# The end of a layer norm in another order: chain to the reciprocal first, means behind it, low parts tile by tile, first new products over two tiles at once

## The chip, the cores and the metric

The kernel runs on one core of one Trainium2 chip. A core has a matrix engine (TensorE, "PE" in the profile), a vector engine (VectorE, "DVE"), an activation engine (ScalarE, "ACT"), a general engine (GpSimd, "POOL") and a queue that only issues transfers (SyncE, "SP"). Each engine works through its own queue in order, and the engines wait for each other by semaphores. The metric is the device time of one execution in microseconds; smaller is better.

## The reference

One inference step of a streaming encoder for two request groups, 256 new frames of one stream and 64 frames of another, of width 1024. Each of two layers computes, with the same weights for both groups:

```python
x = layer_norm(ALPHA * x + 0.5 * swiglu(x, f1_w1, f1_w2), ln1_g, ln1_b)
z = x @ w_in                      # latents, band q k v, gates
...                               # latent attention and chunked band attention
mix = (sigmoid(g_a) * (o_a @ w_pa) + sigmoid(g_b) * (o_b @ w_pb)) @ w_out
x = layer_norm(ALPHA * x + mix, ln2_g, ln2_b)
x = layer_norm(ALPHA * x + 0.5 * swiglu(x, f2_w1, f2_w2), ln3_g, ln3_b)
```

```python
def layer_norm(x, g, b):
    mu = mean(x); var = mean((x - mu) ** 2)
    return (x - mu) * rsqrt(var + NORM_EPS) * g + b
```

All in float32. So there are six layer norms in a row of dependent stages, and nothing behind a norm can be computed wholly before it.

## The kernel before

**Layout.** The 320 frames (64 + 256) lie along the free axis and the 1024 features along the partitions, in eight tiles of 128 x 320. A mean over the features is therefore a product with a matrix of ones divided by 1024 (`self.ones`), which leaves the mean in every partition.

**Three products for one.** Each float32 factor is split into a high part in a shorter format that the matrix engine takes at full rate and a low part, the rest. `mm3` (L125) makes one product of a weight block and an activation tile from three: high with high, high weight with low activation, low weight with high activation.

**Weights.** All weights come in one stream of 128 x 128 blocks in the order of use (`WeightStream`, L49). A transfer on SP's queue brings eight blocks; ACT casts them to the high part `whi` (L81) and DVE subtracts to get `wlo` (L82). Each call of `next` keeps three chunks loaded and two split ahead. Eight blocks feed 24 products. The order of the blocks in memory is recorded from the order of the calls.

**A layer norm** (`layer_norm`, L309) has the tiles of ALPHA*x + f(x) in `d[0..7]`, made one after the other by `produce(m)`. All values are shifted by a first estimate `c` of the mean, taken from tile 0. `S` sums the tiles and `Q` their squares. `finished(m)` makes, for all but the last norm, a "raw" pair (high and low part of d times the gain, not normalised), then squares the tile on ACT and adds it to `Q` on DVE.

**The group.** While mean and variance are worked out, PE multiplies the raw pairs with the weights of the next stage's first six output tiles (`ffn_group`, L220, or `mix_group`, L232; six accumulators, 8 x 6 x 3 = 144 products). Two added columns of the raw pairs carry gain and bias, so that `finish` (L242) can correct the results later: `fin = (md * u + ps) * rstd` on DVE, with `u` copied out of the accumulator.

**The end of a norm** before the change, in the order of the source: the group's first step (18 products with raw tile 0); `pm` and `pq`, the products of ones with `S` and `Q`; `msq` (square of `pm`, ACT); the variance and its clamp (DVE L384, L385); the square root (ACT L386); the reciprocal (DVE L387); `md`, a copy of `pm`; the other steps of the group; the mean taken off all eight tiles (DVE L396, read from the accumulator `pm`); then for each tile the scaling by gain and reciprocal (DVE L399), the high part `xhi` with the bias (ACT L404) and the low part `xlo` (DVE L405). The last norm makes no raw pairs and no low parts; it writes its tiles out, and POOL takes the mean off three of them.

**Behind the norm.** `ffn` evacuates the group's three pairs of accumulators (`evac`, with `finish`) and multiplies the other 19 pairs from `xhi` and `xlo`, in each pair first all eight blocks of one accumulator and then those of the other. `attention` takes the group's results as band q, band k and latent kv, and starts with the four tiles of band v (`w_in("bv", i, "mm")`). It also adds `xhi` and `xlo` on POOL for the next residual (`residual`, L305), which the FFN does on DVE.

**Accumulators.** Eight banks in two pools of four, tagged "mm" and "at". The group holds three of each; `pm` takes the fourth "at" and `pq` the fourth "mm".

**The order on each engine** is planned when the program is built: a planner places the instructions by priority, which is the order of the source, as soon as its own estimate of times says that their inputs are ready. `high_priority()` moves what stands inside it ahead. `order(ins, after)` (L110) adds an edge that only holds for this planning and makes no semaphore: `ins` is placed behind `after` on its queue.

Of the kernel before, what the change touches and what calls it, by code (L numbers as in the profile page):

```python
# [8 lines left out]
F32 = mybir.dt.float32  # L9
F32R = mybir.dt.float32r  # L10
AF = mybir.ActivationFunctionType
ALU = mybir.AluOpType
# [3 lines left out]
T = 320  # L16
# [3 lines left out]
KD = D // P  # L20
# [14 lines left out]
TR = T + 2  # L35
# [65 lines left out]
class Model:  # L101
# [23 lines left out]
    def mm3(self, out, w, x, start, stop):  # L125
        self.mm(out, w[0], x[0], start, False)
        self.mm(out, w[0], x[1], False, False)
        self.mm(out, w[1], x[0], False, stop)

    def scratch(self, name="t"):  # L130
        return self.sc.tile([P, T], F32, tag="t", name=name)
# [88 lines left out]
    def ffn_group(self, l, f):  # L220
        NG = 3
        grp = [[self.psum("mm"), self.psum("at")] for _ in range(NG)]

        def step(k, x, n):
            for p in range(NG):
                for j in range(2):
                    w = self.ws.next(("w1", l, f, p, j, k))
                    self.mm3(grp[p][j][:, :n], w, x, k == 0, k == KD - 1)

        return grp, step  # L230

    def mix_group(self, l):  # L232
        grp = [self.psum("mm" if j < 3 else "at") for j in range(6)]

        def step(k, x, n):
            for j in range(6):
                what, i = (("bq", 0), ("bk", 0), ("bq", 1), ("bk", 1), ("ckv", 0), ("ckv", 1))[j]
                self.mm3(grp[j][:, :n], self.ws.next((what, l, i, k)), x, k == 0, k == KD - 1)

        return grp, step  # L240

# [12 lines left out]
    def ffn(self, l, f, pre):  # L254
        tc, nc, ws = self.tc, self.nc, self.ws
        which = 1 if f == 1 else 3
        last = l == DEPTH - 1 and which == 3
        with tc.tile_pool(name="h", bufs=1, reuse_waits="tile") as hp, \
# [18 lines left out]
            grp = pre  # L277
# [2 lines left out]
            self.raw_pre = True  # L280
            for p in range(len(grp), KF):
                pair = (self.psum("mm"), self.psum("at"))
                for j in range(2):
                    for k in range(KD):
                        w = ws.next(("w1", l, f, p, j, k))
                        self.mm3(pair[j][:, :T], w, (self.xhi[k], self.xlo[k]), k == 0, k == KD - 1)
                evac(p, *pair, False)

            def produce(m):
# [19 lines left out]
    def layer_norm(self, l, which, dd, sums, raw, produce, ys, group):  # L309
# [3 lines left out]
        nc = self.nc  # L313
        last = group is None
        c, S, Q = sums
# [8 lines left out]
                nc.gpsimd.tensor_copy(raw[m][0][:, T:TR], self.csth[:, g])  # L324
                nc.gpsimd.tensor_copy(raw[m][1][:, T:TR], self.cstl[:, g])

        def finished(m):

            if not last:
                g = gain[m][0]  # L330
                nc.scalar.activation(raw[m][0][:, :T], d[m], AF.Copy, scale=g)
                nc.vector.scalar_tensor_tensor(raw[m][1][:, :T], d[m], g, raw[m][0].bitcast(F32)[:, :T], ALU.mult, ALU.subtract)
            if m == 0:
                nc.scalar.activation(Q, d[0], AF.Square)
            elif not (last and m == KD - 1):
                q = self.scratch("sq")
                nc.scalar.activation(q, d[m], AF.Square)
                nc.vector.tensor_tensor(Q, Q, q, ALU.add)

        ps = produce(0)  # L340
        nc.vector.scalar_tensor_tensor(d[0], d[0], scale, ps[:, :T], ALU.mult, ALU.add)
# [7 lines left out]
        finished(0)  # L349
        for m in range(1, KD):  # L350
# [4 lines left out]
            if m == KD - 1:  # L355
                nc.vector.tensor_tensor(S, S, d[m], ALU.add)
                nc.vector.tensor_tensor(S, S, ps[:, :T], ALU.add)
            nc.vector.tensor_tensor(d[m], d[m], ps[:, :T], ALU.add)
            if m < KD - 1:
                nc.vector.tensor_tensor(S, d[0] if m == 1 else S, d[m], ALU.add)  # L360
            finished(m)
        sq = None
        if last:
            sq = self.scratch("sq")
            nc.scalar.activation(sq, d[KD - 1], AF.Square)
        else:
            grp, step = group()
            step(0, raw[0], TR)
        pm = self.psum("at", "pm")
        pq = self.psum("mm", "pq")  # L370
        self.mm(pm[:, :T], self.ones, S, True, True)
        self.mm(pq[:, :T], self.ones, Q, True, not last)
        if last:
            self.mm(pq[:, :T], self.ones, sq, False, True)
        md, v = self.md, self.rstd
        msq = self.scratch("msq")
        if not last:
            warm = self.scratch("warm")
            nc.scalar.activation(warm[:, 0:2], self.ones[:, 0:2], AF.Sqrt)
        nc.scalar.activation(msq, pm[:, :T], AF.Square)  # L380
        if last:
            nc.vector.scalar_tensor_tensor(v, pq[:, :T], eps, msq, ALU.add, ALU.subtract)
        else:
            nc.vector.tensor_tensor(v, pq[:, :T], msq, ALU.subtract)  # L384
            nc.vector.tensor_scalar(v, v, 0.0, eps, ALU.max, ALU.add)  # L385
        nc.scalar.activation(v, v, AF.Sqrt)  # L386
        nc.vector.reciprocal(v, v)  # L387
        nc.scalar.copy(md, pm[:, :T])
        if not last:
            for k in range(1, KD):  # L390
                step(k, raw[k], TR)
        for m in range(KD):
            if last and m in (4, 5, 6):
                nc.gpsimd.tensor_tensor(d[m], d[m], md, ALU.subtract)
            else:
                nc.vector.tensor_tensor(d[m], d[m], pm[:, :T], ALU.subtract)  # L396
        for m in (0, 1, 2, 3, 7, 4, 5, 6) if last else range(KD):
            g, b = gain[m]
            nc.vector.scalar_tensor_tensor(d[m], d[m], g, v, ALU.mult, ALU.mult)  # L399
            if last:  # L400
                nc.scalar.activation(d[m], d[m], AF.Identity, bias=b)  # L401
                nc.sync.dma_start(out=self.a["y"][:, m, :], in_=d[m])
            else:
                nc.scalar.activation(self.xhi[m], d[m], AF.Identity, bias=b)  # L404
                nc.vector.scalar_tensor_tensor(self.xlo[m], d[m], b, self.xhi[m].bitcast(F32), ALU.add, ALU.subtract)  # L405
        return None if last else grp


    def mixer(self, l, pre):
# [29 lines left out]
class Mixer:  # L439
# [328 lines left out]
    def attention(self, pre):  # L768
# [265 lines left out]
```

## Time and profile before

| | |
|---|---|
| time, median of 3 runs | 1524.67 us (1524.53 to 1528.79) |
| the profiled execution, its own time | 1524.2 us |
| its span, first to last instruction | 1522.4 us |
| granted clock of the matrix engine, mean | 0.990 |
| products | 10204 |

The page gives the time by engine, the chain of work that ended last, and the costliest groups of instructions; a line number is that of the listing above, and all products have the line of `mm` (L108). In a row of the timeline stand start, length, engine, line, operation, output and inputs, shapes, count, and in brackets how long the engine had been idle and what released it. In a row of the stretches stand the stretch, its length, the busy time of each engine with its instructions, the clock granted to PE, the share of the transfer engines and GB/s. In a row of the waits stand who waited for whom, how long in total, how often, and the longest.

### The profile page before, as it was taken

What the parts mean: (1) busy time and instruction counts of PE and PEld (TensorE: products, weight loads), DVE (VectorE), ACT (ScalarE), POOL (GpSimd) and SP (SyncE); (2) the same over time, 40 slices, a digit from 0 to 9 for tenths busy, and PEclk for the clock granted to TensorE, in tenths of its full rate; (3) what the DMA queues carried; (4) which work ended last, traced back from release to release, by engine and by line L of the source; (5) the groups of instructions that cost most, each with busy time, mean ns of one, the idle gap of its engine ahead of it and who ended that gap; (6) DMA issues with size and microseconds to landing.
All of it is one profiled execution on the core that took longest, in us unless ns stands there. A gap on an engine that the chain in (4) does not pass through costs nothing.

```text
span 1522.4 us, 25515 instructions
## 1 busy us (share of the span) xinstructions
PE 1488.9 (98%) x10204; PEld 1453.5 (95%) x10204; DVE 932.7 (61%) x1571; ACT 713.4 (47%) x1190; POOL 105.6 (7%) x194
## 2 busy tenths in 40 slices
PE   9999999999999989999999999999999998999996
PEld 9999999999899989999999999989998998999996
DVE  6444558774566884446595445597655579744454
ACT  5344334665444554444454444357634445444332
POOL 2000002231002000000010000042110000000000
PEclk9999999999999999999999999999999999999998
DMA  7544443854234434454444544457352254444541
GB/s 244 150 152 152 148 147 123 256 152 130 88 97 126 152 111 150 144 150 152 153 141 150 152 152 145 149 156 223 126 148 83 84 153 139 126 152 152 151 144 59
DMA packets 69910, 219.37 MB, mean 144 GB/s; under 512 B 8416, under 2 KB 17568, under 8 KB 69792
## 3 DMA queue, kind: packets, MB, share of 16 engines
q1 hardware_dynamic: 69792, 217.75, 46.4%
q8 instruction: 80, 1.31, 0.4%
q14 instruction: 38, 0.31, 0.1%
HBM read 211.74 MB, written 4.67 MB: 142 GB/s over the span
## 4 chain that ended last, share of the span: by engine, by line
PE 95%; DVE 3%; ACT 1%; issue 0%; DMA 0%; ACTq 0%; DVEq 0%
PE ps L108 89%; PE sp L108 1%; PE po L108 1%; PE ss L108 1%; DVE d L399 1%; DVE wlo L82 1%; DVE xlo L405 1%; PE st L549 0%; DVE rstd L387 0%; ACT d L401 0%; DVE d L396 0%; DMA wst<-in_w_dram 0%; PE pt L556 0%; PE st L552 0%; PE pt L555 0%
## 5 line engine op out<-in xcount | busy, mean ns | idle before, releaser
L82 DVE TENSOR_TENSOR wlo<-wst,whi 128x1024 fp32r<-128x1024 f32 (+1 forms) x387 | 471.7, 1220 | 384.6 <-ACT whi L81 382.9
L81 ACT CAST whi<-wst 128x1024 fp32r<-128x1024 f32 (+1 forms) x387 | 402.4, 1041 | 495.4 <-PE ps L108 233.6
L108 PE MATMUL ps<-xhi,whi 128*128 128x320 f32 x1760 | 548.8, 313 | 11.5 <-DVE fin L249 5.8
L108 PE MATMUL ps<-xlo,whi 128*128 128x320 f32 x1760 | 549.0, 312 | 6.7 <-DVE xlo L405 6.7
L108 PE MATMUL ps<-xhi,wlo 128*128 128x320 f32 x1760 | 545.0, 311 | 0.0
L108 PEld LDWEIGHTS ps<-xhi,whi 128*128 128x128 f32 x1760 | 333.2, 190 | 13.8 <-issue 6.8
L108 PEld LDWEIGHTS ps<-xlo,whi 128*128 128x128 f32 x1760 | 333.6, 190 | 9.5 <-DVE xlo L405 8.5
L108 PEld LDWEIGHTS ps<-xhi,wlo 128*128 128x128 f32 x1760 | 332.8, 190 | 0.6 <-issue 0.5
L108 PE MATMUL ps<-hh,whi 128*128 128x320 f32 x704 | 217.6, 309 | 0.0
L108 PE MATMUL ps<-hh,wlo 128*128 128x320 f32 x704 | 217.5, 309 | 0.0
L108 PE MATMUL ps<-hl,whi 128*128 128x320 f32 x704 | 217.5, 309 | 0.0
L108 PEld LDWEIGHTS ps<-hh,whi 128*128 128x128 f32 x704 | 132.2, 188 | 0.0
L108 PEld LDWEIGHTS ps<-hh,wlo 128*128 128x128 f32 x704 | 132.1, 188 | 0.0
L108 PEld LDWEIGHTS ps<-hl,whi 128*128 128x128 f32 x704 | 132.1, 188 | 0.0
L138 ACT CAST hh<-h 128x320 fp32r<-128x320 f32 x88 | 39.9, 456 | 62.0 <-DVE h L273 57.2
L273 DVE TENSOR_TENSOR h<-silu,ps 128x320 f32<-128x320 f32 x79 | 38.0, 484 | 49.0 <-PE ps L108 49.0
L145 DVE TENSOR_TENSOR hl<-h,hh 128x320 fp32r<-128x320 f32 x88 | 42.5, 488 | 17.5 <-ACT hh L138 17.4
L272 ACT ACTIVATE silu<-ps 128x320 f32<-128x320 f32 x79 | 33.9, 433 | 25.7 <-PE ps L108 25.7
L108 PE MATMUL ps<-rawl,whi 128*128 128x322 f32 x144 | 45.5, 316 | 0.0
L108 PE MATMUL ps<-rawh,whi 128*128 128x322 f32 x144 | 45.4, 315 | 0.0
L108 PE MATMUL ps<-rawh,wlo 128*128 128x322 f32 x144 | 44.7, 311 | 0.0
L108 PE MATMUL ps<-raw,whi 128*128 128x322 f32 x192 | 44.3, 316 | 0.0
(247 smaller groups left out, 1794.7 us busy)
## 6 DMA issues: line engine op xcount, KB each, us to landing
wst<-in_w_dram SPq DMA_DIRECT2D x382, 512.0 KB, 3.5
K<-in_ckT_dram SPq DMA_DIRECT2D x8, 256.0 KB, 4.7
vc<-in_cv_dram SPq DMA_DIRECT2D x8, 256.0 KB, 5.1
T<-in_E_dram SPq DMA_DIRECT2D x16, 128.0 KB, 3.9
xin<-in_x_dram SPq DMA_DIRECT2D x8, 160.0 KB, 5.7
out_kb_dram<-K SPq DMA_DIRECT2D x8, 160.0 KB, 3.7
out_vb_dram<-vt SPq DMA_DIRECT2D x8, 160.0 KB, 5.0
out_y_dram<-d SPq DMA_DIRECT2D x8, 160.0 KB, 1.9
```

Of the source, the lines that this page charges most:

```text
L81: self.nc.scalar.copy(hi[:, a:b], t[:, a:b])
L82: self.nc.vector.tensor_tensor(lo[:, a:b], t[:, a:b], hi.bitcast(F32)[:, a:b], ALU.subtract)
L108: return self.nc.tensor.matmul(out, lhsT, rhs, start=start, stop=stop)
L138: self.nc.scalar.copy(out, src)
L145: eng.tensor_tensor(out, src, hi.bitcast(F32), ALU.subtract)
L272: nc.scalar.activation(s, pa[:, :T], AF.Silu)
L273: nc.vector.tensor_tensor(h, s, pg[:, :T], ALU.mult)
L399: nc.vector.scalar_tensor_tensor(d[m], d[m], g, v, ALU.mult, ALU.mult)
L405: nc.vector.scalar_tensor_tensor(self.xlo[m], d[m], b, self.xhi[m].bitcast(F32), ALU.add, ALU.subtract)
```

## The change

The end of `layer_norm` is reordered; the computation stays the same.

- `finished(m)` is divided into `raw_part(m)` and `square(m)`. For the last tile the sum `S`, the tile itself and its square (with the sum `Q`) come first, at high priority, and the raw part behind them.
- `pm`, `pq`, the warming of the square root's table, `md`, `msq`, variance, clamp, square root and reciprocal are at high priority. `pq` is placed behind the last product of the group's first step (`step` and `mm3` return it). `msq` is the square of `md`, no longer of `pm`.
- The mean is taken off with `md` in place of `pm` (all norms but the last), and from the third tile on (in the last norm from the first) it is placed behind the clamp (`begun`).
- Scaling, high part and low part follow tile by tile: the scaling of tile m is placed behind the low part of tile m-2.
- The first pair of products behind the group in `ffn` goes through the eight tiles of x once, with both accumulators in turn, and so do the first two tiles of band v in `attention`.

```diff
     def mm3(self, out, w, x, start, stop):
...
-        self.mm(out, w[1], x[0], False, stop)
+        return self.mm(out, w[1], x[0], False, stop)
...
                 pair = (self.psum("mm"), self.psum("at"))
-                for j in range(2):
-                    for k in range(KD):
-                        w = ws.next(("w1", l, f, p, j, k))
-                        self.mm3(pair[j][:, :T], w, (self.xhi[k], self.xlo[k]), k == 0, k == KD - 1)
+                both = [(j, k) for k in range(KD) for j in range(2)] if p == len(grp) else [(j, k) for j in range(2) for k in range(KD)]
+                for j, k in both:
+                    w = ws.next(("w1", l, f, p, j, k))
+                    self.mm3(pair[j][:, :T], w, (self.xhi[k], self.xlo[k]), k == 0, k == KD - 1)
...
-        def finished(m):
-
+        def raw_part(m):
             if not last:
                 g = gain[m][0]
                 nc.scalar.activation(raw[m][0][:, :T], d[m], AF.Copy, scale=g)
                 nc.vector.scalar_tensor_tensor(raw[m][1][:, :T], d[m], g, raw[m][0].bitcast(F32)[:, :T], ALU.mult, ALU.subtract)
...
+        def square(m):
+            q = Q if m == 0 else self.scratch("sq")
+            nc.scalar.activation(q, d[m], AF.Square)
+            if m and not (last and m == KD - 1):
                 nc.vector.tensor_tensor(Q, Q, q, ALU.add)
+            return q
...
+        m = KD - 1
+        ps = produce(m)
+        nc.vector.tensor_tensor(S, S, d[m], ALU.add)
+        with self.tc.high_priority():
+            nc.vector.tensor_tensor(S, S, ps[:, :T], ALU.add)
+            nc.vector.tensor_tensor(d[m], d[m], ps[:, :T], ALU.add)
+            sq = square(m)
+        raw_part(m)
+        after = None
+        if not last:
             grp, step = group()
-            step(0, raw[0], TR)
+            after = step(0, raw[0], TR)
...
+        with self.tc.high_priority():
+            self.mm(pm[:, :T], self.ones, S, True, True)
+            ins = self.mm(pq[:, :T], self.ones, Q, True, not last)
+            if last:
+                self.mm(pq[:, :T], self.ones, sq, False, True)
+            else:
+                self.order(ins, after)
+                warm = self.scratch("warm")
+                nc.scalar.activation(warm[:, 0:2], self.ones[:, 0:2], AF.Sqrt)
+            nc.scalar.copy(md, pm[:, :T])
+            nc.scalar.activation(msq, md, AF.Square)
+            if last:
+                begun = nc.vector.scalar_tensor_tensor(v, pq[:, :T], eps, msq, ALU.add, ALU.subtract)
+            else:
+                nc.vector.tensor_tensor(v, pq[:, :T], msq, ALU.subtract)
+                begun = nc.vector.tensor_scalar(v, v, 0.0, eps, ALU.max, ALU.add)
+            nc.scalar.activation(v, v, AF.Sqrt)
+            nc.vector.reciprocal(v, v)
         if not last:
             for k in range(1, KD):
                 step(k, raw[k], TR)
...
-                nc.vector.tensor_tensor(d[m], d[m], pm[:, :T], ALU.subtract)
...
+                ins = nc.vector.tensor_tensor(d[m], d[m], pm[:, :T] if last else md, ALU.subtract)
+                if last or m >= 2:
+                    self.order(ins, begun)
...
+        low = []
+        for m in range(KD):
+            g, b = gain[m]
+            ins = nc.vector.scalar_tensor_tensor(d[m], d[m], g, v, ALU.mult, ALU.mult)
+            if m >= 2:
+                self.order(ins, low[m - 2])
+            nc.scalar.activation(self.xhi[m], d[m], AF.Identity, bias=b)
+            low.append(nc.vector.scalar_tensor_tensor(self.xlo[m], d[m], b, self.xhi[m].bitcast(F32), ALU.add, ALU.subtract))
+        return grp
...
+        two = [M.psum("mm"), M.psum("at")]
+        for k in range(KD):
+            for i in range(2):
+                M.mm3(two[i][:, :T], ws.next(("bv", l, i, k)), self.x[k], k == 0, k == KD - 1)
         pv = [M.psum("at") for _ in rows]
         for i in range(NPAIR):
-            ps = self.w_in("bv", i, "mm")
+            ps = two[i] if i < 2 else self.w_in("bv", i, "mm")
```

More of the change, by code (lines that the diff above doesn't have):

```diff
@@ L227, in step @@
                     w = self.ws.next(("w1", l, f, p, j, k))
-                    self.mm3(grp[p][j][:, :n], w, x, k == 0, k == KD - 1)
+                    ins = self.mm3(grp[p][j][:, :n], w, x, k == 0, k == KD - 1)
+            return ins
         return grp, step
@@ L237, in step @@
                 what, i = (("bq", 0), ("bk", 0), ("bq", 1), ("bk", 1), ("ckv", 0), ("ckv", 1))[j]
-                self.mm3(grp[j][:, :n], self.ws.next((what, l, i, k)), x, k == 0, k == KD - 1)
+                ins = self.mm3(grp[j][:, :n], self.ws.next((what, l, i, k)), x, k == 0, k == KD - 1)
+            return ins
         return grp, step
@@ L332, in finished @@
                 nc.vector.scalar_tensor_tensor(raw[m][1][:, :T], d[m], g, raw[m][0].bitcast(F32)[:, :T], ALU.mult, ALU.subtract)
[L333 to L337, printed above, removed]
+        def square(m):
+            q = Q if m == 0 else self.scratch("sq")
+            nc.scalar.activation(q, d[m], AF.Square)
+            if m and not (last and m == KD - 1):
                 nc.vector.tensor_tensor(Q, Q, q, ALU.add)
+            return q
         ps = produce(0)
@@ L348, in layer_norm @@
         nc.vector.tensor_tensor(d[0], d[0], c, ALU.subtract)
-        finished(0)
-        for m in range(1, KD):
+        raw_part(0)
+        square(0)
+        for m in range(1, KD - 1):
             if last and m == KD - 2:
@@ L354, in layer_norm @@
             ps = produce(m)
-            if m == KD - 1:
-                nc.vector.tensor_tensor(S, S, d[m], ALU.add)
-                nc.vector.tensor_tensor(S, S, ps[:, :T], ALU.add)
             nc.vector.tensor_tensor(d[m], d[m], ps[:, :T], ALU.add)
[L359 to L366, printed above, removed]
+            nc.vector.tensor_tensor(S, d[0] if m == 1 else S, d[m], ALU.add)
@@ L367, in layer_norm @@
+            raw_part(m)
+            square(m)
+        m = KD - 1
[5 more added lines that the diff above has]
+            sq = square(m)
+        raw_part(m)
+        after = None
+        if not last:
             grp, step = group()
-            step(0, raw[0], TR)
+            after = step(0, raw[0], TR)
@@ L369, in layer_norm @@
         pm = self.psum("at", "pm")
         pq = self.psum("mm", "pq")
[L371 to L374, printed above, removed]
         md, v = self.md, self.rstd
         msq = self.scratch("msq")
[L377 to L388, printed above, removed]
+        with self.tc.high_priority():
[16 more added lines that the diff above has]
+            nc.vector.reciprocal(v, v)
@@ L395, in layer_norm @@
             else:
[L396 to L400, printed above, removed]
+                ins = nc.vector.tensor_tensor(d[m], d[m], pm[:, :T] if last else md, ALU.subtract)
+                if last or m >= 2:
+                    self.order(ins, begun)
+        if last:
+            for m in (0, 1, 2, 3, 7, 4, 5, 6):
+                g, b = gain[m]
+                nc.vector.scalar_tensor_tensor(d[m], d[m], g, v, ALU.mult, ALU.mult)
                 nc.scalar.activation(d[m], d[m], AF.Identity, bias=b)
                 nc.sync.dma_start(out=self.a["y"][:, m, :], in_=d[m])
[L403 to L406, printed above, removed]
+            return None
+        low = []
+        for m in range(KD):
+            g, b = gain[m]
+            ins = nc.vector.scalar_tensor_tensor(d[m], d[m], g, v, ALU.mult, ALU.mult)
[4 more added lines that the diff above has]
+        return grp
     def mixer(self, l, pre):
```

## The prediction

> **What bounds the kernel now.** I read the page first, then the waits of the matrix engine (PE), then the timeline around each of the six norms.
>
> ```profile
> PE 1488.9 (98%) x10204; PEld 1453.5 (95%) x10204; DVE 932.7 (61%) x1571; ACT 713.4 (47%) x1190; POOL 105.6 (7%) x194
> PE 95%; DVE 3%; ACT 1%; issue 0%; DMA 0%; ACTq 0%; DVEq 0%
> 5.01 169.42 PE ps L108 x1150
> ```
>
> The first row is the busy time by engine, the second the chain that ended last by engine, the third one piece of that chain: start, length, what. PE is the bound: 169.42 us for 1150 products is 0.147 us a product, and no product is added or removed by the change. Only the holes in PE's work can be won. I number the norms N1 to N6 in order of time; N1 and N4 hand over to the mixers, N2 and N5 to the second FFNs, N3 to the next layer, N6 ends the kernel. The waits of PE, asked for one norm at a time (us in total, times, longest), are for N1
>
> ```profile
> PE ps L108 <- DVE xlo L405: 2.2, 1, 2.2
> PE ps L108 <- DVE fin L249: 1.2, 1, 1.2
> ```
>
> for N2
>
> ```profile
> PE ps L108 <- ACT xhi L404: 3.8, 1, 3.8
> PE ps L108 <- DVE xlo L405: 3.1, 1, 3.1
> ```
>
> for N4
>
> ```profile
> PE ps L108 <- DVE fin L249: 1.8, 1, 1.8
> PE ps L108 <- DVE xlo L405: 1.5, 4, 0.4
> ```
>
> and for N5
>
> ```profile
> PE ps L108 <- DVE fin L249: 2.8, 1, 2.8
> PE ps L108 <- ACT xhi L404: 1.7, 1, 1.7
> ```
>
> N3 has none. They sum to 3.4, 6.9, 3.3 and 4.5, so 18.1 us. Behind each hole the granted clock falls. The stretches by window show it (length, PE busy, granted clock, DMA, GB/s):
>
> ```profile
> 266.00:272.00 6.00, 4.82 (x17) 0.50 0.94 306
> 544.00:549.00 5.00, 4.59 (x18) 0.53 0.00 0
> 1023.00:1027.00 4.00, 4.00 (x19) 0.57 0.06 15
> 1294.00:1300.00 6.00, 5.50 (x21) 0.53 0.28 89
> ```
>
> Busy time times the missing share of the clock gives 4.82 x 0.50 = 2.4, then 2.2, 1.7 and 2.6: 8.9 us. So N1 costs 5.8, N2 9.1, N4 5.0, N5 7.1, N3 nothing: **27.0 us is all there is to win**, 1.8% of the time. The Trainium skill's page "TensorE: Matmul & The Clock Gate", Part 1, puts the fall to half clock behind an idle window of about 3.4 us; the 3.8 us hole of N2 agrees, but N4 lost its clock with no hole above 1.8 us, so here the measurement decides and thinly filled stretches count too.
>
> **What the waits are made of.** N2 shows the chain best. The products from the unnormalised tiles (the group of 144) end at 536.7; the next ones need xhi and xlo.
>
> ```profile
> 524.06 0.56 ACT L331 ACTIVATE raw<-d,cst 128x320 fp32r<-128x320 f32 x1
> 525.34 0.55 DVE L332 SCALAR_TENSOR_TENSOR raw<-d,cst,raw 128x320 fp32r<-128x320 f32 x1
> 525.80 0.48 DVE L338 TENSOR_TENSOR gt<-gt,sq 128x320 f32<-128x320 f32 x1
> 528.88 3.27 DVE L396 TENSOR_TENSOR d<-d,pm 128x320 f32<-128x320 f32 x8
> 529.92 0.70 PE L108 MATMUL pq<-gt,ones 128*128 128x320 f32 x2
> 532.07 0.48 DVE L384 TENSOR_TENSOR rstd<-pq,msq 128x320 f32<-128x320 f32 x1
> 532.47 1.22 DVE L82 TENSOR_TENSOR wlo<-wst,whi 128x1024 fp32r<-128x1024 f32 x1
> 533.96 0.47 ACT L386 ACTIVATE rstd<-rstd 128x320 f32<-128x320 f32 x1 [1.61 <-DVE rstd L385]
> 535.03 2.14 DVE L387 RECIPROCAL rstd<-rstd 128x320 f32<-128x320 f32 x1
> 536.38 0.31 PE L108 MATMUL ps<-raw,wlo 128*128 128x322 f32 x1
> 539.31 3.78 DVE L399 SCALAR_TENSOR_TENSOR d<-d,cst,rstd 128x320 f32<-128x320 f32 x8
> 540.50 0.85 PE L108 MATMUL ps<-xhi,whi 128*128 128x320 f32 x4 [3.81 <-ACT xhi L404]
> 543.81 3.78 DVE L405 SCALAR_TENSOR_TENSOR xlo<-d,cst,xhi 128x320 fp32r<-128x320 f32 x8
> ```
>
> VectorE (DVE) takes off eight means before it may form the variance, scales all eight tiles before it makes the first low part, and in between splits weights. Over the hole itself the stretches show PE, PE's loads, DVE, ACT and POOL:
>
> ```profile
> 536.00:540.00 4.00, 0.69 (x5) 0.43 (x3) 4.00 (x10) 0.56 (x5) 0.00 (x0) 1.00 0.22 73
> ```
>
> DVE is busy for all 4.00 us. The stage is bound by DVE's queue, and the change only reorders that queue.
>
> **The change part by part.**
>
> *Last tile first.* The raw parts of tile 7 go behind its square. ACT's 0.56 and DVE's 0.55 leave the way to the last sum of squares: about 1.0 us (on DVE instructions follow each other every 0.46 us). The raw parts are read last by the group, whose 144 products last 21 us: hidden. The matrix products pm and pq may now stand right behind the group's first 18 products; where the plan puts them earlier than S and Q are ready, PE waits, at most the time from there to Q. I take nothing, because the plan has placed pq at 529.92, over three microseconds behind the Q that ended at 526.28: the plan is the later of the two. pq comes 1.0 us earlier.
>
> *Means behind the chain.* Eight means (3.27) leave the way between pq and the variance. pq is done at 530.62 and the variance began at 532.07, so 1.3 us are won there, with the 1.0 above 2.3. The square now reads md, not pm: one copy of 0.42 stands in the chain, but pm is multiplied before pq, and the 1.05 us of copy and square fit beside the 1 to 3 us between them. The weight split between variance and clamp costs 1.13 and may or may not move out: the reciprocal ends 2.3 to 3.4 us earlier, at 533.7 to 534.8 in place of 537.1. Then the means follow: one fits into the hole of the square root, seven remain, 7 x 0.40 = 2.8. The split that stood there (1.13) stays. Scaling of N2 starts at 537.6 to 538.7 in place of 539.31. **Most of what the chain wins is paid back to the means**, since both are on DVE.
>
> *Low parts tile by tile.* Now xlo of tile 0 follows scaling 0 and 1 by some 1.3 us, where it came 4.5 us later. From the first scaling to the last low part DVE needs 16 x 0.46 = 7.4 us and two splits, 2.3: 9.7 us, whichever order. New waits come with this: the scaling of tile m stands behind the low part of m-2, which waits for ACT's xhi of m-2. Queued behind it on DVE are the next scalings, splits and the fins of the group, and PE waits for all of them.
>
> *Two tiles at once.* Over two tiles PE takes 6 x 0.147 = 0.88 us per tile of x in place of 0.44, nearly DVE's 0.92. In the mixers both start in the free accumulators of pm and pq, so the second no longer needs a fin: that wait (1.2, 1.8; in N5 2.8) goes, until the third product asks for one 7 us later. Accumulators are freed as early, as the means no longer read pm. The order of the weights in memory follows the order of use; the issues on SP's queue keep their number and size.
>
> *Sums.* N2: scaling starts at 538.2 (middle), last low part 9.7 later, PE's last tile 0.9 behind: 548.8; without holes it were 536.7 + 48 x 0.147 = 543.7. Loss 5.1, with a little slow clock 5.5: **gain 3.6**. For N5 and N1 the same terms are set against their own rows:
>
> ```profile
> 1285.45 2.15 DVE L387 RECIPROCAL rstd<-rstd 128x320 f32<-128x320 f32 x1 [0.54 <-ACT rstd L386]
> 1291.13 0.56 PE L108 MATMUL ps<-xhi,whi 128*128 128x320 f32 x2 [1.67 <-ACT xhi L404]
> ```
>
> N5: the reciprocal ended at 1287.5; 2.3 to 3.4 earlier, with the means and one split behind it, scaling starts at 1288.1 to 1289.2. PE's last tile is done 10.6 later, 1299.2 in the middle. The group ended at 1289.5 (1291.13 less the hole of 1.67), so without holes it were 1296.6. Loss 2.7, with some slow clock 3.0: **gain 4.1**.
>
> ```profile
> 249.53 2.15 DVE L387 RECIPROCAL rstd<-rstd 128x320 f32<-128x320 f32 x1 [0.54 <-ACT rstd L386]
> 257.51 5.36 DVE L405 SCALAR_TENSOR_TENSOR xlo<-d,cst,xhi 128x320 fp32r<-128x320 f32 x6
> 260.51 0.31 PE L108 MATMUL ps<-xhi,whi 128*128 128x320 f32 x1
> ```
>
> ```profile
> L405 DVE SCALAR_TENSOR_TENSOR xlo<-d,cst,xhi x40: 535/548/1174, 257.5 to 1298.0; 128x320 fp32r<-128x320 f32 x40
> L307 POOL TENSOR_TENSOR d<-xhi,xlo 128x320 f32<-128x320 f32 x16 | 20.2, 1293 | 37.9 <-DVE xlo L405 37.5 <-DVE u L246 0.4
> ```
>
> N1: the reciprocal ended at 251.6, so scaling starts at 252.7 in the middle and the first low part comes at 254.0, in place of 257.5. But POOL adds xhi and xlo of the same tiles for the mixer's residual (1.29 us each), and beside it a low part takes 1174 ns in place of 548. Undisturbed the last low part would come at 252.7 + 9.7 + 1.1 (a third split) = 263.5, before PE asks for it at 260.5 + 7 x 0.88 = 266.7. With eight adds each holding DVE up by 0.63 (1174 less 548) or, if scalings suffer too, 1.2, it comes at 268.5 to 273. I take the lower end and some slow clock: loss 3.0 of 5.8, **gain 2.8**; N4 alike, 2.6 of 5.0, **gain 2.4**. N3 has no hole and no POOL beside it: 0.
>
> ```profile
> 1510.46 0.89 DVE L396 TENSOR_TENSOR d<-d,pm 128x320 f32<-128x320 f32 x2 [1.28 <-ACT md L388]
> 1511.27 0.48 DVE L382 SCALAR_TENSOR_TENSOR rstd<-pq,msq 128x320 f32<-128x320 f32 x1
> 1511.67 1.27 DVE L396 TENSOR_TENSOR d<-d,pm 128x320 f32<-128x320 f32 x3
> ```
>
> N6: the variance can start at most 0.8 earlier, by the two means ahead of it; these two go behind the reciprocal (0.8), of the other three one or two stay in the hole of the square root, and the square waits for the copy of md. Scaling starts where it did or 0.6 later: **minus 0.3.**
>
> 3.6 + 4.1 + 2.8 + 2.4 - 0.3 = 12.6. The profiled execution took 1524.2 (span 1522.4 and 1.8 around it), the median of the runs is 1524.67: 1524.7 - 12.6 = **1512**.
>
> **Rivals.**
> *A, all holes go* (about 1500): the splits, 1.13 each, slip out of the way of chain and low parts, three or four of them in a norm, and the clock stays up; 24 of the 27 us. Against it: DVE's sum above exceeds PE's time in N2 by itself.
> *B, POOL and DVE block each other* (about 1519): adds on POOL and scalings and low parts on DVE now alternate tile by tile, from the first low part on, 3.5 us earlier than now. At 1.2 us per add N1 and N4 win nothing, and N2 and N5 keep 3 us each: 1524.7 - 6 = 1519. The 1174 ns speak for it. It is also what the Trainium skill says on the page "SBUF: State Buffer", section "Who interferes with whom": a DVE instruction with two SBUF inputs contends with GpSimd reading SBUF, and whoever starts first holds the shared port; the trace agrees (1174 against 548). By that rule the means, which now read md in SBUF and no longer PSUM, could be hit as well; no POOL work lies beside them here.
> *C, no effect* (1520 to 1529): the plan orders by its own estimate of when things are ready, and may put splits and means where they were; DVE's total is the same and the last low part comes when it came.
> *D, the alternating order stalls DVE* (about 1530):
>
> ```profile
> ACT whi L81 <- PE ps L108: 233.6, 168, 3.1
> ```
>
> ACT's queue is in order, and its weight casts wait for PE to free a buffer, 168 times, up to 3.1 us. An xhi behind such a cast now stops its low part, and with it every later scaling, where eight scalings ran freely before. Five norms with one such hold each pay back the 12.6 us at 2.5 us a hold; with two holds of 1.8 the change loses 5 us. For it: casts and xhi share one queue in each norm. Against it: PE asks for a tile only every 0.88 us, so a hold that DVE has made up in N1, N3 and N4 before the group ends costs nothing.
>
> **How the numbers follow.** Forecast (1506 to 1516) 0.44, A 0.12, B (1516 to 1520) 0.15, C 0.18, D 0.11. A measurement of this kernel tells about 0.3% from no change, here 4.6 us: faster (under 1520.1) 0.71, same 0.18, slower (over 1529.2) 0.11. The range leaves out D, the fast half of A and the slow half of C: 1500 to 1524.
>
> **What would show it.** Right: pq within 6 us of the sum of squares in each norm, the eight means behind the reciprocal on DVE, xlo and scaling in turns, PE's waits for fin gone in N1 and N4, PE's waits in N2 under 5 us in many short pieces. Wrong: a PE wait for S or Q ahead of pm or pq; waits of xlo on xhi above 1 us (D); L405 and L399 with means above 800 ns (B); new waits in N3.

## The result, and the profile after

| | before | after |
|---|---|---|
| time, median of 4 runs | 1525.48 us (1524.53 to 1528.79) | 1511.36 us (1508.83 to 1511.93) |
| the profiled execution, its own time | 1524.2 us | 1511.78 us |
| its span | 1522.4 us | 1510.0 us |

The ratio is 0.990, with a 95% interval of 0.9881 to 0.992: the medians lie 14.1 us apart, at a forecast of 1512 us, which was 12.6 us under the 1524.7 of the first three runs. The profiled execution of the kernel before was a little faster than its four timed runs, so the gains read from profiles, here and below, mostly come out smaller than those of the medians (here 12.6 against 14.1). The page of the changed kernel answers to the first two rows of the page before:

```profile
PE 1483.7 (98%) x10204; PEld 1448.7 (96%) x10204; DVE 931.5 (62%) x1571; ACT 713.7 (47%) x1190; POOL 98.2 (7%) x194
PE 92%; ACT 3%; DVE 3%; DMA 1%; issue 1%; SPq 0%; ACTq 0%; DVEq 0%
```

The work is the same, but PE's share of the chain that ended last fell from 95% to 92%, while ACT's rose from 1% to 3% and DMA's from nothing to 1%. A faster kernel with less of its bound engine in the chain has traded some holes for others. PE's waits in the changed kernel, asked for N1, N2, N4 and N5 in turn (N4 has no row):

```profile
PE ps L108 <- DVE fin L251: 0.7, 1, 0.7
...
PE ps L108 <- ACT xhi L419: 2.6, 1, 2.6
...
PE ps L108 <- DVE fin L251: 1.0, 1, 1.0
PE ps L108 <- DVE xlo L420: 0.4, 1, 0.4
```

That is 0.7, 2.6, 0 and 1.4 us in place of 3.4, 6.9, 3.3 and 4.5. But in mixer 1, 31 and 49 us behind the first products from N4's tiles (at 1037.05 and 1054.37, against 1005.55), stand two waits, where mixer 1 of the kernel before had one of 1.1 us, for `pt`:

```profile
PE po L108 <- ACT pt L577: 3.2, 1, 3.2
PE sp L108 <- DVE pp L621: 1.0, 1, 1.0
```

**Where the time went.** Both programs run the same 10204 products. The start of PE's n-th product in the trace before, less the start of the n-th after, is what has been won up to there. Read at a product ahead of each norm, behind it, and behind the mixers' attention, that gives the table below (us; the first line is the forecast; "rest" holds what lies ahead of N1 and at N6):

| | N1 | mixer 0 | N2 | N3 | N4 | mixer 1 | N5 | rest | sum |
|---|---|---|---|---|---|---|---|---|---|
| forecast | 2.8 | 0 | 3.6 | 0 | 2.4 | 0 | 4.1 | -0.3 | 12.6 |
| after | 5.6 | -1.6 | 4.1 | 0.0 | 6.2 | -6.2 | 5.5 | -0.9 | 12.6 |

The sums agree to the tenth, and the parts do not; that the sums agree so closely is luck, for another execution of the same kernel (f1 below) gives 13.4. The norms win 21.4 us, 8.5 more than forecast for the four, and 7.8 are given back in the mixers, a place of which the prediction says nothing. So two things were open: why N1 and N4 win all they had to lose although GpSimd adds beside their low parts, and why mixer 1 gives back just what N4 wins. In mixer 1 the waits of ACT, PE's stretch (length, PE, loads, DVE, ACT and POOL busy, granted clock, DMA, GB/s) and ACT's timeline are

```profile
ACT whi L81 <- DMA wst<-in_w_dram: 7.1, 3, 4.9
```

```profile
1052.00:1060.00 8.00, 5.63 (x27) 4.77 (x28) 6.08 (x11) 5.24 (x15) 1.85 (x3) 0.79 0.85 225
```

```profile
1034.06 1.05 ACT L81 CAST whi<-wst 128x1024 fp32r<-128x1024 f32 x1 [4.87 <-DMA wst<-in_w_dram]
...
1047.84 1.05 ACT L81 CAST whi<-wst 128x1024 fp32r<-128x1024 f32 x1 [1.37 <-DMA wst<-in_w_dram]
...
1053.75 0.56 ACT L577 COPY pt<-pt 128x512 f32<-128x512 f32 x1
```

ACT stands 4.87 us for a chunk of weights (before, 0.2 us in the whole mixer), and the exponentials and the copy `pt` behind it in its queue are late with it (how much, the second group shows). The weights are late because their transfers were issued late. SP's queue:

```profile
1003.73 10.60 SPq L67 DMA_DIRECT2D wst<-in_w_dram  x3
1014.39 0.90 SPq L788 DMA_DIRECT2D cst<-in_cckv_dram  x2
...
1027.47 1.64 SPq L67 DMA_DIRECT2D wst<-in_w_dram  x3
```

Between the two weight loads, 13.1 us, stand 22 other transfers (the latent cache, K, vc and T of the banded attention, the stores of keys and values; an expectation below says 24).

### The profile page after: what moved, and what is told of

It is laid out like the page before. It is cut to its first block, busy times and chain, and to the rows that moved or that the text cites. A ratio compares the mean times of both kernels' runs of the same rounds, so it can differ in the third digit from the quotient of the medians.

```text
span 1510.0 us, 25510 instructions
## 1 busy us (share of the span) xinstructions
PE 1483.7 (98%) x10204; PEld 1448.7 (96%) x10204; DVE 931.5 (62%) x1571; ACT 713.7 (47%) x1190; POOL 98.2 (7%) x194
## 4 chain that ended last, share of the span: by engine, by line
PE 92%; ACT 3%; DVE 3%; DMA 1%; issue 1%; SPq 0%; ACTq 0%; DVEq 0%
PE ps L108 87%; PE po L108 1%; PE sp L108 1%; PE ss L108 1%; DMA wst<-in_w_dram 1%; DVE wlo L82 1%; ACT whi L81 0%; DVE d L403 0%; PE st L564 0%; ACT pp L549 0%; DVE rstd L395 0%; DVE xlo L420 0%; DVE d L416 0%; ACT L549 0%; ACT L632 0%
## 5 line engine op out<-in xcount | busy, mean ns | idle before, releaser
L82 DVE TENSOR_TENSOR wlo<-wst,whi 128x1024 fp32r<-128x1024 f32 (+1 forms) x387 | 472.3, 1222 | 375.4 <-ACT whi L81 373.8
L108 PE MATMUL ps<-xhi,whi 128*128 128x320 f32 x1760 | 540.7, 311 | 4.9 <-ACT xhi L419 2.6
L108 PEld LDWEIGHTS ps<-xhi,whi 128*128 128x128 f32 x1760 | 329.5, 188 | 7.4 <-ACT xhi L419 2.9
```

Source lines behind the costliest of these rows:

```text
L82: self.nc.vector.tensor_tensor(lo[:, a:b], t[:, a:b], hi.bitcast(F32)[:, a:b], ALU.subtract)
L108: return self.nc.tensor.matmul(out, lhsT, rhs, start=start, stop=stop)
```

## The experiments

Each run was timed in rounds with the kernel before on the same chip (its medians 1525.6 to 1526.5). The gains by place are worked out as above, from one profiled execution each. Theory P is the prediction's own sum; theory M says that the mixers take back what the norms win, through weights that come late.

### First group: the change taken apart, and the bands' loads on another queue

**e1, one tile after the other.**

```diff
-                both = [(j, k) for k in range(KD) for j in range(2)] if p == len(grp) else [(j, k) for j in range(2) for k in range(KD)]
+                both = [(j, k) for k in range(KD) for j in range(2)] if False else [(j, k) for j in range(2) for k in range(KD)]
...
-        two = [M.psum("mm"), M.psum("at")]
-        for k in range(KD):
-            for i in range(2):
-                M.mm3(two[i][:, :T], ws.next(("bv", l, i, k)), self.x[k], k == 0, k == KD - 1)
...
-            ps = two[i] if i < 2 else self.w_in("bv", i, "mm")
+            ps = self.w_in("bv", i, "mm")
```

> Only the order of the products that follow a norm is put back to one tile after the other (first pair of every FFN1, first two bv tiles of the mixers); the rest is as in the changed kernel. With one tile at a time the products can end no sooner than the last low part plus 0.44 us plus the 3.5 us of the second tile; with two they end 0.88 us behind the last low part: 3.1 us apart, at each of N1, N2, N4, N5. Theory P (the prediction's sum: low parts limit PE at all four, and the mixers keep what the norms win): about +12 us, 1523 us. Theory M (mixer 1 takes back whatever N4 wins, here by weights that come late): N4's part costs nothing at the end, +9 us, 1520 us, and PE is 6 us less ahead at the start of mixer 1 but as far ahead at its end. Rival T (the earlier reciprocal alone made the gain): at most 1513 us.

**e2, scalings and low parts free.**

```diff
             ins = nc.vector.scalar_tensor_tensor(d[m], d[m], g, v, ALU.mult, ALU.mult)
-            if m >= 2:
-                self.order(ins, low[m - 2])
```

> Only the order of scalings and low parts is set free: on VectorE's queue the eight scalings of a norm then stand ahead of its eight low parts, as in the kernel before. The first low part comes 7 x 0.40 = 2.8 us later, the last one at the same time. Theory P and theory M: the products over two tiles take 0.88 us a tile, so they start 2.8 us later and then run without waits, where they were held to about 1.0 us a tile: 1 to 2 us lost at N2 and N5, 1 at N1 (a little less for M, where N4's loss is hidden): 1514 to 1517 us. Rival T: the low parts' end decides, no change, 1511 us.

**e3, means free.**

```diff
-                if last or m >= 2:
+                if last:
                     self.order(ins, begun)
```

> Only the order that holds six of the means behind the variance is dropped: all eight then stand ahead of it on VectorE's queue. The reciprocal ends 6 x 0.40 = 2.4 us later, but the eight means are done then: the first scaling starts 0 to 0.5 us later, since the means had to be done anyhow. Theory P (paid back to the means): within 1.5 us of the changed kernel, 1511 to 1513 us. Rival T (the reciprocal's time sets all that follows): +2.4 us at each of N1, N2 and N5, 1518 us.

**e4, the bands' loads on GpSimd's queue.**

```diff
     def band_load(self, i):
...
-        nc.sync.dma_start(out=K[:, 0:PAST], in_=a["ckT"][l, i])
+        nc.gpsimd.dma_start(out=K[:, 0:PAST], in_=a["ckT"][l, i])
...
-        nc.sync.dma_start(out=vc, in_=a["cv"][l, i])
+        nc.gpsimd.dma_start(out=vc, in_=a["cv"][l, i])
```

(and the four loads of T in the same way)

> Only the queue of the transfers that load K, vc and T of the banded attention is changed, from SyncE's to GpSimd's; on SyncE's queue the weight loads then stand between the stores of the new keys and values instead of behind 24 other transfers. Theory M (mixer 1 gives N4's 6.2 us back, and mixer 0 1.7 us of N1's, because the weights' transfers are issued too late): ScalarE's wait for wst in mixer 1 (7.1 us) goes, and 4 to 8 us of the time: 1503.5 to 1507.5 us. Rival A (the softmax chain sets mixer 1: exponentials, table loads and copies on ScalarE and what VectorE does between them): the waits for pt stay, 1510 to 1513 us. Rival G (GpSimd's queue with its slower issue and its memsets of T gets in the way): over 1513 us.

| | time (us) | ratio, interval | N1 | mixer 0 | N2 | N4 | mixer 1 | N5 | rest |
|---|---|---|---|---|---|---|---|---|---|
| e1 | 1513.67 | 0.9917 (0.9900 to 0.9933) | 0.4 | -0.7 | 3.6 | 3.4 | -0.5 | 5.5 | -2.0 |
| e2 | 1518.44 | 0.9948 (0.9933 to 0.9963) | 5.6 | -4.1 | 1.1 | 3.2 | -1.7 | 2.5 | -0.9 |
| e3 | 1518.95 | 0.9952 (0.9937 to 0.9967) | 5.6 | -5.5 | 3.9 | 6.1 | -4.2 | 2.6 | -0.3 |
| e4 | 1506.21 | 0.9868 (0.9853 to 0.9883) | 5.6 | 0.7 | 4.7 | 6.3 | -0.9 | 5.5 | -0.9 |

e1 came out nearest to its rival's time, for another reason: with the old order of products N1 wins next to nothing and N4 half, while N2 and N5 keep nearly all; but mixer 1 then gives back only 0.5, so most of that loss does not reach the end. e2 is slower than expected: the alternating order is worth 3 us at each of N2, N4 and N5. At N5 PE waits for the low parts again:

```profile
PE ps L108 <- DVE xlo L418: 3.1, 1, 3.1
```

(e2's wait at N5; L418 is the low part). e3 falls on the side of its rival: with all eight means ahead of the variance N5 wins 2.9 us less, N2 0.2 less and N1 the same. At N5 this is not the price of the means alone: in e3's trace a weight split, too, stands again between variance and clamp there (1277.41, 1.22 us), as it did at N2 in the kernel before. That mixer 0 gives back 5.5 us was in neither expectation and is not explained. e4 came out as theory M has it, 1506 us, with both mixers keeping what they get. That looked like a verdict for SP's queue, but GpSimd's queue had been changed too: the residual's adds, in order behind the new transfers, had moved away from the low parts.

### Second group: each suspect alone, on the kernel before where possible

**f1** is the changed kernel again. **f2** puts the two tiles at once alone (as in the change) on the kernel before; **f3** puts e4's edit on it. **f4**, on the changed kernel:

```diff
-        M.residual(self.d, nc.gpsimd)
+        M.residual(self.d, nc.vector)
```

> The changed kernel again, as the common base of this group of runs: every theory expects 1511 us, with 1 us for another chip.

> The kernel before with one part of the change alone: the first products over two tiles at once. Theory M: at N1 and N4 the accumulators that the fins were to free are free already, and PE asks for a tile only every 0.88 us; 5 us won at N1 and 3 at N4, of which mixer 0 takes back 1.7 and mixer 1 all 3; under 1 at N2 and N5: 3 to 4 us in sum, 1521.5 to 1522.5 us. Theory P (a gain only where the wait for fin goes, 1.2 and 1.8 us at N1 and N4 and 2.8 at N5, kept to the end): 1519 us. Rival S (without the alternating order the first low part comes 3 us later and PE waits for it whichever way the products are ordered): under 1 us, 1525 us.

> The kernel before with the loads of K, vc and T on GpSimd's queue. Theory M (weights came in time in the kernel before, since PE stood at N1 and N4 meanwhile; the weights are late only for a PE that arrives 6 us earlier, with the weight loads planned behind the stores of the values): PE's losses in mixer 1 were 2.1 us before, so 0 to 2.5 us: 1523 to 1526 us. Rival Q (fewer transfers on SyncE's queue are worth the same 5 us in any kernel): 1520 us.

> The changed kernel with the adds of the mixer's residual on VectorE instead of GpSimd; in VectorE's queue they stand behind the last low part and two thirds of the fins. Theory P (GpSimd's adds hold up the low parts and cost 3.0 us at N1 and 2.6 at N4): 3 to 5.6 us won at the two norms. Theory M (the low parts get faster, 842 to some 540 ns, but PE does not wait for them there: it lost 0.9 us at N1 and nothing at N4): at most 1 us won at the norms, and 8 x 0.46 = 3.7 us more on VectorE ahead of the first scores, of which 0 to 4 us come out at the end: 1511 to 1515 us.

| | time (us) | ratio, interval | N1 | mixer 0 | N2 | N4 | mixer 1 | N5 | rest |
|---|---|---|---|---|---|---|---|---|---|
| f1 | 1511.61 | 0.9903 (0.9888 to 0.9918) | 5.6 | -2.7 | 4.1 | 6.2 | -4.4 | 5.5 | -0.9 |
| f2 | 1516.76 | 0.9937 (0.9922 to 0.9952) | 5.6 | -1.5 | -0.4 | 5.0 | -0.8 | -0.6 | -0.4 |
| f3 | 1513.63 | 0.9918 (0.9903 to 0.9933) | 5.0 | 0.4 | -0.1 | 5.5 | 0.0 | 0.5 | -1.0 |
| f4 | 1505.43 | 0.9869 (0.9852 to 0.9886) | 5.6 | -0.6 | 4.7 | 6.3 | -0.7 | 5.5 | -1.0 |

f2 shows that two tiles at once win N1 and N4 alone, and nothing at N2 and N5: 2.2 us faster than theory P had it, and 5 us faster than theory M. f3 fells theory M as it stood: in the kernel before, where weights were not late, the bands' loads on another queue win 12 us, and they win them *at the norms* N1 and N4. The groups of DVE and POOL around N4 tell why. Before, then f3:

```profile
L405 DVE SCALAR_TENSOR_TENSOR xlo<-d,cst,xhi 128x320 fp32r<-128x320 f32 x8 | 7.5, 973 | 0.0
L82 DVE TENSOR_TENSOR wlo<-wst,whi 128x1024 fp32r<-128x1024 f32 x3 | 4.4, 1465 | 0.0
...
L307 POOL TENSOR_TENSOR d<-xhi,xlo 128x320 f32<-128x320 f32 x8 | 10.0, 1285 | 19.0 <-DVE xlo L405 19.0
```

```profile
L405 DVE SCALAR_TENSOR_TENSOR xlo<-d,cst,xhi 128x320 fp32r<-128x320 f32 x8 | 4.1, 544 | 0.0
L82 DVE TENSOR_TENSOR wlo<-wst,whi 128x1024 fp32r<-128x1024 f32 x3 | 3.7, 1218 | 0.0
```

In f3 no add of POOL lies in that window, a low part takes 544 ns in place of 973, and the hole is gone. So GpSimd's adds *were* the hole at N1 and N4 before, as the prediction assumed. f4 asks the same of the changed kernel. Its time, 6 us under f1, is near what theory P expected, but not at the places it named: N1 and N4 win no more than they did, and the mixers give back 1.3 us in place of 7.8 (in f1 7.1), with the weight loads still behind the same block of transfers on SP's queue. Around N4, the changed kernel, then f4:

```profile
L420 DVE SCALAR_TENSOR_TENSOR xlo<-d,cst,xhi 128x320 fp32r<-128x320 f32 x8 | 6.1, 766 | 0.0
L82 DVE TENSOR_TENSOR wlo<-wst,whi 128x1024 fp32r<-128x1024 f32 x4 | 6.0, 1492 | 0.0
...
L251 DVE SCALAR_TENSOR_TENSOR fin<-md,u,ps 128x320 f32<-128x320 f32 x6 | 2.9, 536 | 0.0
...
L309 POOL TENSOR_TENSOR d<-xhi,xlo 128x320 f32<-128x320 f32 x8 | 8.6, 1077 | 24.0 <-DVE xlo L420 24.0
```

```profile
L82 DVE TENSOR_TENSOR wlo<-wst,whi 128x1024 fp32r<-128x1024 f32 x4 | 4.9, 1222 | 0.1
L420 DVE SCALAR_TENSOR_TENSOR xlo<-d,cst,xhi 128x320 fp32r<-128x320 f32 x8 | 4.4, 546 | 0.0
```

This is **theory K**: beside the adds DVE loses 8 x 0.22 us in the low parts and 4 x 0.27 in the weight splits, 2.8 us at N4. (The second step of `fin`, with two inputs in SBUF, is slowed too, 860 against 489 ns, three times in that window; that 1.1 us lies behind the split which is followed here.) PE does not wait for it at the norm any more, so the delay travels on: the split ends later, frees its staging buffer later, and SP, which waits for that buffer, starts its 22 transfers and the weight loads behind them later. First SP's wait for the splits (changed kernel, 996 to 1030 us), then rows of DVE and PE in the changed kernel, and of PE, DVE and SP in f4:

```profile
SPq L67 <- DVE wlo L82: 16.5, 4, 5.6
```

```profile
1012.77 1.21 DVE L82 TENSOR_TENSOR wlo<-wst,whi 128x1024 fp32r<-128x1024 f32 x1
```

```profile
1005.55 0.31 PE L108 MATMUL ps<-xhi,whi 128*128 128x320 f32 x1
```

```profile
1004.09 0.31 PE L108 MATMUL ps<-xhi,whi 128*128 128x320 f32 x1
```

```profile
1008.91 1.22 DVE L82 TENSOR_TENSOR wlo<-wst,whi 128x1024 fp32r<-128x1024 f32 x1
```

```profile
1001.15 9.34 SPq L67 DMA_DIRECT2D wst<-in_w_dram  x3
1010.54 0.90 SPq L788 DMA_DIRECT2D cst<-in_cckv_dram  x2
```

The rows of PE are the first products from normalised tiles, 1005.55 in the changed kernel and 1004.09 in f4. From there the split ends 8.4 us later in the one (1013.98) and 6.0 in the other (1010.13), and SP's block starts 8.8 (1014.39) and 6.4 us later (1010.54): 2.4 of the 2.8 us that the adds cost DVE arrive at SP. ACT's wait for weights in mixer 1 is 7.1 us in the one and

```profile
ACT whi L81 <- DMA wst<-in_w_dram: 2.4, 2, 1.6
```

in the other. What ACT loses at that wait is seen from the copy ahead of it, the cast behind it and the copy `pt` that PE waits for. The changed kernel first (its cast and its `pt` are shown above), then f4:

```profile
1028.77 0.42 ACT L510 COPY K<-ps 128x320 f32<-128x320 f32 x1 [0.43 <-PE ps L108]
```

```profile
1027.18 0.42 ACT L510 COPY K<-ps 128x320 f32<-128x320 f32 x1 [0.43 <-PE ps L108]
1028.40 1.05 ACT L81 CAST whi<-wst 128x1024 fp32r<-128x1024 f32 x1 [0.79 <-DMA wst<-in_w_dram]
1048.29 0.56 ACT L577 COPY pt<-pt 128x512 f32<-128x512 f32 x1
```

Ahead of the wait the changed kernel is 1.6 us behind f4, little more than the 1.5 us by which it came to N4 later (1005.55 against 1004.09); the cast behind the wait comes 5.7 us later and `pt` 5.5. So in these two traces the delay enters ACT's queue at the wait for weights. GpSimd's own lateness is no rival: the waits of neither trace have a row in which an engine waits for POOL between 1005 and 1075 us.

The Trainium skill's page "SBUF — State Buffer", section "Who interferes with whom", names the lock behind it: a DVE instruction with two SBUF inputs contends with a GpSimd instruction that reads SBUF. The traces agree. `fin`, with one input in the accumulator, keeps its 536 ns beside the adds, and the weight splits, with two inputs in SBUF, do not. Who is held up is seen on the timelines of DVE and POOL in the changed kernel:

```profile
1004.09 0.54 DVE L416 SCALAR_TENSOR_TENSOR d<-d,cst,rstd 128x320 f32<-128x320 f32 x1
1004.56 1.16 DVE L420 SCALAR_TENSOR_TENSOR xlo<-d,cst,xhi 128x320 fp32r<-128x320 f32 x1
...
1004.25 1.12 POOL L309 TENSOR_TENSOR d<-xhi,xlo 128x320 f32<-128x320 f32 x1 [1.63 <-DVE xlo L420]
```

The scaling has begun when the add comes and keeps its 0.54 us; the low part that comes next takes 1.16.

### Third group: theory K put to the test

**g1** is f4's edit on the kernel before, with nothing of the change. **g2** is f4 with e1's edit, **g3** f4 with e4's. **g4**, on the changed kernel:

```diff
-                tc.tile_pool(name="wst", bufs=3) as wst, \
+                tc.tile_pool(name="wst", bufs=4) as wst, \
...
-            self.ws = WeightStream(nc, a["w"], wst, wsp, 3, 2)
+            self.ws = WeightStream(nc, a["w"], wst, wsp, 4, 2)
```

> The kernel before with the adds of the mixer's residual on VectorE, nothing of the change. Theory K (GpSimd's adds hold each VectorE instruction beside them up by some 0.55 us; in the kernel before that makes the holes at N1 and N4, and in the changed kernel the same loss is carried into the mixers): 5 us won at N1 and 5 at N4, as with the bands' loads on GpSimd, which also moved the adds away from the low parts: 1514 to 1516.5 us. Rival T (there it was the transfers' queue that mattered, not the adds): N1 and N4 keep their holes, 1523 us or more. Rival D (8 x 0.41 = 3.3 us more on VectorE are as bad as the hold-up): 1519 us or more.

> The changed kernel with the residual's adds on VectorE and the first products put back to one tile after the other. Theory K (two tiles at once wins at N1 and N4 only because it asks for the low parts at half the pace while GpSimd's adds hold them up): without the adds it is worth at most 1 us at each of N1 and N4, and 1.6 us at N2 and N5 as in the run with the order of products put back: 1505.5 to 1509 us against 1505.4 us with two tiles. Rival O (the order of products is worth 5 us at N1 and 3 at N4 by itself, through the accumulators that need no fin): 1512 us or more.

> The changed kernel with both: the residual's adds on VectorE and the loads of K, vc and T on GpSimd's queue. Theory K (the adds are the cause, SyncE's queue only passes the delay on to the weights): little is left to win in the mixers, 1504 to 1506.5 us. Rival M (SyncE's order of transfers is a cause by itself): the gains add up, 1499 to 1502.5 us.

> The changed kernel with a fourth staging buffer for weights, loaded four chunks ahead instead of three; GpSimd's adds stay beside the low parts, and on SyncE's queue the three weight loads still stand behind the bands' loads, with one more load ahead of them. Theory K with its middle link (the adds delay the weight splits on VectorE, these free the staging buffers late, so SyncE starts the bands' transfers and the next weights late, and ScalarE then waits for weights): the wait for wst in mixer 1 (7.1 us) falls under 2 us and the mixers keep 3 to 6 us more: 1505 to 1508.5 us. Rival V (VectorE's lateness itself, with splits and scores behind it, takes the lead away, whenever the weights come): 1510 us or more.

| | time (us) | ratio, interval | N1 | mixer 0 | N2 | N4 | mixer 1 | N5 | rest |
|---|---|---|---|---|---|---|---|---|---|
| g1 | 1515.51 | 0.9935 (0.9921 to 0.9950) | 5.0 | -0.2 | -0.8 | 5.5 | -1.4 | 0.8 | 0.2 |
| g2 | 1506.96 | 0.9878 (0.9863 to 0.9892) | 5.3 | -0.7 | 3.6 | 5.4 | 0.0 | 5.3 | -2.1 |
| g3 | 1504.25 | 0.9861 (0.9846 to 0.9876) | 5.6 | 0.1 | 4.1 | 6.3 | -0.3 | 5.5 | -0.8 |
| g4 | 1509.20 | 0.9893 (0.9868 to 0.9919) | 5.6 | -6.3 | 4.7 | 6.2 | -0.7 | 5.5 | -1.0 |

g1, g2 and g3 came out where theory K put them. One word in the kernel before, the engine of eight adds a layer, wins 10 us (g1), and PE's wait at N4 shrinks to one:

```profile
PE ps L108 <- DVE fin L249: 0.5, 1, 0.5
```

Without the adds the order of the first products is worth 0.3 us at N1 and 0.9 at N4 (g2 against f4), where with the adds it was worth 5.2 and 2.8 (e1 against after). Moving the bands' loads as well adds 1.2 us (g3 against f4, on two chips and with intervals that overlap), where rival M asked for 3 to 6: no effect of SP's order is shown once the adds are gone. g3 is the fastest kernel of the study, and its mixer 1 shows no wait of PE that is listed.

g4 settles nothing. Mixer 1 keeps its lead as the middle link would have it, but its wait for weights is still 4.1 us, and mixer 0 gives back 6.3 us; its four runs lie from 1506.6 to 1513.3, across both expectations. That the delay reaches PE *through the weights* rests on the traces of f4 and the changed kernel above, one execution each, not on a run of its own. Mixer 0 was not followed in this way.

## Why the prediction was right in its sum and wrong in its parts

- **Bound and total.** Right: the products are the same, only holes could be won, and 21.4 of the 27.0 us were won at the norms. One term of the ceiling was too small: N4 was given 5.0 us to lose and won 6.2.
- **Chain first.** `pq` starts 3.7 to 4.1 us after the start of the last sum of squares in all norms but the last, inside the six; but it was 3.7 to 4.1 in the kernel before as well, so this sign told nothing. With PE's lead taken off, `pq` came 0.4 to 0.6 us earlier at N1, N2, N4 and N5, not 1.0. The reciprocal, forecast 2.3 to 3.4 us earlier, came only 0.4 earlier at N2 (530.85 against 535.03, less the 3.8 by which the whole kernel was ahead there) and 1.4 to 1.5 at N1 and N5. The plan put six means (and at N2 a split) between clamp and reciprocal, and none behind it, where the prediction wanted all eight: the chain's gain was spent before the reciprocal. DVE at N2 in the changed kernel:

```profile
527.06 0.33 DVE L393 TENSOR_SCALAR rstd<-rstd 128x320 f32<-128x320 f32 x1
527.30 2.49 DVE L403 TENSOR_TENSOR d<-d,md 128x320 f32<-128x320 f32 x6
529.72 1.22 DVE L82 TENSOR_TENSOR wlo<-wst,whi 128x1024 fp32r<-128x1024 f32 x1
530.85 2.15 DVE L395 RECIPROCAL rstd<-rstd 128x320 f32<-128x320 f32 x1
534.39 1.00 DVE L416 SCALAR_TENSOR_TENSOR d<-d,cst,rstd 128x320 f32<-128x320 f32 x2
```

  First scaling at N2: 534.39 + 3.8 = 538.2, as forecast; at N1 and N5 it came 1.5 earlier than forecast. In sum "paid back to the means" holds, but e3 shows that their place, with that of a split, is worth more than nothing, 2.9 us at N5.
- **Low parts tile by tile.** Worth 3.0 us at each of N2 and N5 (e2), most of what these norms win.
- **Two tiles at once, and the step that failed.** The prediction let PE walk through the eight tiles at 0.88 us each and so stand for the last low part, 7 x 0.88 us after its start. The planner did not: counted in the order of PE's instructions, 65 products at N1, 94 at N2, 81 at N4 and 97 at N5 stand between the first product of normalised tiles and the first that needs the last low part, against 42 in the prediction and 22, 40, 22 and 40 before. The others are products of further output tiles with the early tiles (a third at N1, and more at the others). At 0.147 us that is 9.6 to 14.3 us of cover in place of 6.2. So at N2 the last low part ended at 548.3, with the lead 552.1 on the clock of before, 4 us *later* than the 547.9 forecast (the group's `fin` now stand between the low parts), and N2 still won 4.1 us against 3.6 forecast. That this number is near is luck too. The forecast left a loss of 5.5 us at N2 for the end of the low parts; PE did lose 5.2 us, but at the first products, which wait for the first `xhi`, and nothing at the last low part:

```profile
535.58 1.26 PE L108 MATMUL ps<-xhi,whi 128*128 128x320 f32 x4 [2.63 <-ACT xhi L419]
```

- **GpSimd's adds** hold up DVE, but less than the 0.63 us an add of the prediction's lower end: on the mean 0.43 us a low part at N4 before and 0.22 after, and 0.25 to 0.27 a split. A low part that is hit still loses 0.62 us (1.16 against 0.54), but in the changed kernel only three of the eight at N4 are. The losses of 3.0 and 2.6 us left at N1 and N4 are the terms that failed, and not because the low parts were early: N1's last one ended at 269.4, inside the 268.5 to 273 forecast. With 9.6 us of cover PE lost 0.9 us at N1 and nothing at N4.
- **The missing term.** "The mixers keep what the norms win" was never written down, only assumed. PE's lead of 14 us behind N4 met a weight stream whose splits the adds had delayed, and 6.2 us went back there, with 1.6 in mixer 0. The two errors, 8.5 us too little at the norms and 7.8 too little loss in the mixers (with 0.6 more outside both, in the column "rest"), cancelled: the total was right by luck. At N6 one sign of being wrong did show, a wait of PE for `S` ahead of `pm` of 0.6 us.
- **Rivals.** C did not happen (the interval ends at 0.992). D did not happen: DVE has no wait of a low part for `xhi` behind any norm. B was half right, its price real but paid elsewhere. A came true at N4, and would have come nearly true in the sum with the adds moved (19.7 us in f4's trace, 20.5 in g3's).

## What to carry to other kernels

A gain worked out at a stage is not a gain at the end: ask what feeds the engine that gets ahead (here splits, staging buffers, an issuing queue in order), and whether that feed is delayed by the very work that the change hides. Matching the n-th product of two traces shows in one line where a lead is won and where it is lost, and a right total can hide two wrong parts. Where two engines slow each other, moving the work to the engine that is held up anyway can be worth as much as a reordering. DVE spends about as long on eight adds (3.3 us in f4) as it lost beside them, but there they stand behind the last low part (ended at 1011.92) and the last `fin` (1015.06), and hold up neither:

```profile
1014.98 3.30 DVE L309 TENSOR_TENSOR d<-xhi,xlo 128x320 f32<-128x320 f32 x8
```

## What the runs showed of the hardware

- Eight adds of 1.1 us each on GpSimd cost DVE 3.9 us at N4 in the changed kernel (eight low parts of 766 against 546 ns, four weight splits of 1492 against 1222, three second steps of `fin` of 860 against 489); the same adds took DVE 3.7 us of its own:

```profile
L307 DVE TENSOR_TENSOR d<-xhi,xlo 128x320 f32<-128x320 f32 x8 | 3.7, 508 | 0.0
```

  (g1 around N4), and still moving them won 6 us in the changed kernel and 10 in the one before.
- Issuing a transfer costs a little more on GpSimd's queue than on SP's: 0.53 to 0.58 us for a load of T (e4) against 0.33 to 0.59, median 0.51 (changed kernel), and for K and `vc` 0.55 against 0.43. Two rows of e4:

```profile
L488 POOL DMA_DIRECT2D T<-in_E_dram x4 | 2.3, 567 | 0.0
L486 POOL DMA_DIRECT2D T<-in_E_dram x4 | 2.2, 538 | 0.0
```

- Two executions of the same program gave back different amounts in the mixers (1.6 and 6.2 us, 2.7 and 4.4) and ended within 0.8 us of each other: the length of the mixers is not fixed here, and one profile of them is one sample.
